# Shifted weight buffers in one layer, stepped and reversed reads on TensorE in the other

## The chip, the cores and the metric

The kernel runs on one core of one Trainium2 chip. Its TensorE (PE) multiplies a stationary operand of 128 columns, which a weight load (PEld) brings in, by a moving operand that streams past it, and adds into PSUM. VectorE (DVE) and ScalarE (ACT) do the elementwise work, and SyncE (SP) issues all the DMAs. The metric is the device time of one execution in microseconds, taken as the median of the runs shown; lower is better.

## The reference

Two layers over x of 256 tokens by 1024 features, all float32, with two residual sums in each. Cut to what matters:

```python
h = rms_norm(x, norm1_g)
q, k, v, iq, ik, iw, a_in, c_in, g_in = split(h @ w_in)      # w_in: 1024 x 9288
y_attn = dsa_attention(rope(norm(q)), rope(norm(k)), v, rope(iq), rope(ik), iw) @ w_attn_out
a = causal_dwconv(a_val * sigmoid(a_gate), conf_conv_w) + conf_conv_b          # 31 taps
y_conf = silu(layer_norm(a)) @ w_conf_out
y_sc = (c_b * causal_dwconv(c_c * c_x, sc_conv_w)) @ w_sc_out                  # 3 taps
x = x + (gate0 * y_conf + gate1 * y_attn + gate2 * y_sc) @ w_o
u = causal_dwconv(rms_norm(x, norm2_g) @ w_up, ffn_conv_w) + ffn_conv_b        # 1024 x 5632
x = x + (silu(u_gate) * u_val) @ w_down                                        # 2816 x 1024
```

## The kernel before

Activations lie with features on the partitions: a tile such as `hh` is 128 x 8 x 256 (partition, block of 128 features, token). Weights arrive as one long stream of chunks of 128 x 2048 floats (1 MB). Each half chunk of 1024 columns, eight weight tiles of 128 columns, is split into two float32r parts: ACT casts the raw half into `wh` (L421, `cast`), and DVE writes the rest, raw less `wh`, into `wl` (L378). There are six buffers of each, `wh_0` to `wh_5` and `wl_0` to `wl_5`, laid out one after the other, and a half is named by its running number (`wh204`). Activations are split in the same way (`hh` and `hl`, `sh` and `sl`, and so on).

A product is three matmuls for each block of 128 features: high weight by high activation, low weight by high activation, high weight by low activation. `fm` (L361 issues them all) writes these, and `pair` makes two output blocks of it (2 x 8 x 3 = 48 matmuls), `single` one (8 x 3 = 24, or 22 x 3 = 66 in the last stage). In these stages the weights are stationary and 256 columns of tokens move. In the stages of `tok` (IQ, KX, V, Q) the roles are swapped: 128 token columns of `hh` or `hl` are stationary and 512, 328 or 256 columns of `wh` or `wl` move.

The stages of a layer, in order, are A (8 pairs; the first of them on `xgh` and `xgl`, before the norm's factor is known, five pairs in layer 0 and three in layer 1, then on `hha` and `hla`), IQ, KX, V, Q, C (8 pairs) with CB (4 pairs), S (4 pairs), G (12 pairs), T (4 pairs), F (4 pairs), O (8 singles), U (22 pairs) and N (8 singles). The attention's own small matmuls (is, qk, tp, po) are put in between. A digit behind the letters is the layer: `F1_0` is the first pair of F in layer 1. `Plan.schedule` lists all instructions ahead of time by due times and estimated costs; each engine then follows its list, and nothing is decided on the chip. `late` in `pair` and `single` puts the last blocks of the contraction at the end, for inputs that come late; in F it stands in the first pair alone. `Norm.finish` writes `hh` (ACT) and `hl` (DVE) for a norm.

Of the kernel before, what the change touches and what calls it, by code (L numbers as in the profile page):

```python
# [9 lines left out]
F32 = mybir.dt.float32  # L10
F32R = mybir.dt.float32r
I32 = mybir.dt.int32
AF = mybir.ActivationFunctionType
ALU = mybir.AluOpType
PSUM = bass.MemoryType.PSUM

P = 128
D = 1024
S = 256
KD = 8  # L20
# [3 lines left out]
FT = 22  # L24
# [6 lines left out]
CHUNK = 2048  # L31
# [26 lines left out]
for _n, _w in (("ident", 128), ("caus0", 128), ("caus1", 256), ("cosq", 32), ("sinq", 32),  # L58
# [9 lines left out]
BANKS = ("pm", "pq", "pa")  # L68
LAYOUT = (["gap40"] + [f"big_{i}" for i in range(8)] + [f"att_{i}" for i in range(2)] + ["kT_0", "vt_0"],
          ["gap16"] + [f"{t}_{i}" for i in range(6) for t in ("wh", "wl")])  # L70
LOADS = {AF.Sigmoid: "sigmoid", AF.Exp: "exp", AF.Silu: "silu"}
LAT = {("dve", "dve"): 127, ("dve", "act"): 130, ("act", "act"): 143, ("act", "dve"): 143,
       ("dve", "pe"): 365, ("act", "pe"): 390, ("pe", "dve"): 198, ("pe", "act"): 198, ("pe", "pe"): 0,
# [62 lines left out]
def ap_of(x):  # L136
    return x.ap() if isinstance(x, View) else x
# [6 lines left out]
class Plan:  # L144
# [166 lines left out]
    def emit(self, tc, pools):  # L311
        order = self.schedule()
        size = {}
        for o in order:
            for b in o.allocs:
                if b.tag not in BANKS:
                    n = int(np.prod(b.shape[1:]))
                    size[b.slot] = max(size.get(b.slot, 0), n)
        first = [t for group in LAYOUT for t in group]
        for slot in first + [t for t in size if t not in first]:  # L320
            if slot.startswith("gap"):
                pools[0].tile([P, int(slot[3:].split("_")[0])], F32, tag=slot, name=slot)
            elif slot in size:
                pools[0].tile([P, size[slot]], F32, tag=slot, name=f"home_{slot}")
        for o in order:
            for b in o.allocs:
                b.tile = pools[b.tag in BANKS].tile(b.shape, b.dtype, tag=b.slot, name=b.name)
            o.fn()


# [1 line left out]
def trunk(ctx: ExitStack, tc: tile.TileContext, xt: bass.AP, wst: bass.AP, prm: bass.AP,  # L332
          cst: bass.AP, out: bass.AP):
    nc = tc.nc
# [5 lines left out]
    G = Plan()  # L340
# [85 lines left out]
    def low(o, full, hi):  # L426
        vtt(o, full, hi.bitcast(F32), ALU.subtract)

    def ks(t):
        return [t[:, k, :] for k in range(KD)]  # L430
# [20 lines left out]
    class Stream:  # L451
# [38 lines left out]
            self.c += 1  # L490
            self.pos = 0

        def tiles(self, n):
            res = []
            for _ in range(n):
                i = 2 * self.c + self.pos // HALF
                o = self.pos % HALF
                h, l = self.get(i)
                res.append((h[:, o:o + P], l[:, o:o + P]))
                self.pos += P  # L500
                if self.pos == widths[self.c]:
                    self.skip()
            return res

    W = Stream()
# [54 lines left out]
    def rsqrt_rows(sq, name):  # L560
# [10 lines left out]
        G.hot = False  # L571
        return r

    def fm(ps, tiles, xh, xl, ka, kb, first, last, group=4, kw=None):
        for a in range(ka, kb, group):
            g = []
            for i in range(a, min(a + group, kb)):
                h, l = tiles[i]
                g.append(mm(ps, h, xh[i], first and i == ka, False, S, kw=kw))
                g.append(mm(ps, l, xh[i], False, False, S, kw=kw))  # L580
            clk["t"] += pe(g, due=clk["t"])
        for a in range(ka, kb, 2 * group):
            g = []
            for i in range(a, min(a + 2 * group, kb)):
                g.append(mm(ps, tiles[i][0], xl[i], False, last and i == kb - 1, S, kw=kw))
            clk["t"] += pe(g, due=clk["t"])

    def pair(name, xh, xl, late=0):
        ps = G.buf([P, 2, S], "pm", name)
        w = [W.tiles(KD) for _ in range(2)]  # L590
        if not late:
            for i in range(2):
                fm(ps[:, i, :], w[i], xh, xl, 0, KD, True, True)
        else:
            cut = KD - late
            for i in range(2):
                fm(ps[:, i, :], w[i], xh, xl, 0, cut, i == 0, False, group=1 if i == 0 else 4, kw="s")
            for i in range(2):
                fm(ps[:, i, :], w[i], xh, xl, cut, KD, False, True, kw="s")
        G.due = clk["t"]  # L600
        return ps
# [15 lines left out]

    def single(name, n, xh, xl, late=0):
        ps = G.buf([P, S], "pm", name)
        w = W.tiles(n)  # L620
        if late:
            fm(ps, w, xh, xl, 0, n - late, True, False)
            fm(ps, w, xh, xl, n - late, n, False, True)
        else:
            fm(ps, w, xh, xl, 0, n, True, True)
        G.due = clk["t"]
        return ps

    def tok(name, xh, xl, n, chunks):
        one = n * 2 <= 512  # L630
        if one:
            t = G.buf([P, 2, n], "pm", name)
            ps = [t[:, b, :] for b in range(2)]
        else:
            t = [G.buf([P, n], "pm", f"{name}_{b}") for b in range(2)]
            ps = t
        per = KD // (2 * chunks)
        for c in range(chunks):
            base = 2 * W.c
            for k0 in range(2 * c * per, 2 * (c + 1) * per, per):  # L640
                h, l = W.get(base + k0 // per - 2 * c)
                g = []
                for k in range(k0, k0 + per):
                    o = k % per * n
                    for b in range(2):
                        sl = slice(b * P, (b + 1) * P)
                        st = k == 0 and (b == 0 or not one)
                        g.append(mm(ps[b], xh[k][:, sl], h[:, o:o + n], st, False, n, kw="s"))
                        g.append(mm(ps[b], xh[k][:, sl], l[:, o:o + n], False, False, n, kw="s"))
                        g.append(mm(ps[b], xl[k][:, sl], h[:, o:o + n], False, k == KD - 1, n, kw="s"))  # L650
                clk["t"] += pe(g, due=clk["t"])
            W.skip()
        G.due = clk["t"]
        return t

    class Norm:
# [28 lines left out]
        def finish(self):  # L685
            self.r = rsqrt_rows(self.sq, self.name)
            self.hh = big(f"hh{self.name}", F32R)
            self.hl = big(f"hl{self.name}", F32R)
            for j in range(KD):
                G.due += 700  # L690
                h = t1(f"h{self.name}_{j}")
                vstt(h, xres[:, j, :], self.g[:, j:j + 1], self.r, ALU.mult, ALU.mult)
                act(self.hh[:, j, :], h, AF.Copy)
                low(self.hl[:, j, :], h, self.hh[:, j, :])

        def deferred(self, ps, name):
            t = t2(name)
# [3 lines left out]
        def pairs(self, n, name, evac):  # L701
            ndef = NDEF[name]
            xh, xl = ks(self.xh), ks(self.xl)
            for j in range(n):
                if j == ndef:
                    xh, xl = ks(self.hh), ks(self.hl)
                if j == 0:
                    G.due = clk["t"] + 1500
                    self.finish()
                if name == "A0" and j < 2:  # L710
                    if j == 0:
                        first = first_pairs(name, xh, xl)
                    ps = first[j]
                else:
                    ps = pair(f"{name}_{j}", xh, xl, late=1 if j == 0 else 0)
                evac(j, ps, self if j < ndef else None)
            return xh, xl
# [32 lines left out]
    for l in range(DEPTH):  # L750
# [34 lines left out]
        xh, xl = norm.pairs(8, f"A{l}", a_evac)  # L785
# [61 lines left out]
        for g in range(4):  # L847
# [9 lines left out]
            n = g - 1  # L857
# [230 lines left out]
def _stream(inp, l):  # L1088
# [4 lines left out]
    def m(x, j):  # L1093
        return x[:, :, j * P:(j + 1) * P].reshape(P, -1)

    parts = []
    for j in range(8):
        parts.append(np.concatenate([m(a, j), m(a, 8 + j)], 1))
    if l == 0:
        four = np.concatenate(parts[:2], 1).reshape(P, 4, KD, P).transpose(0, 2, 1, 3).reshape(P, -1)  # L1100
        parts[:2] = [four[:, :CHUNK], four[:, CHUNK:]]
# [6 lines left out]
    for i in range(4):  # L1108
# [1 line left out]
            j = 2 * i + u  # L1110
            parts.append(np.concatenate([m(c, 8 + j), m(c, 16 + j)], 1))
        parts.append(np.concatenate([m(c, 2 * i), m(c, 2 * i + 1)], 1))
    def square(n):
        w = _blocks(inp[n][l])
        for i in range(4):
            parts.append(np.concatenate([m(w, 2 * i), m(w, 2 * i + 1)], 1))

    square("w_sc_out")
    for n in (1, 2, 0):
        for i in range(4 * n, 4 * n + 4):  # L1120
            parts.append(np.concatenate([m(g, 2 * i), m(g, 2 * i + 1)], 1))
    for n in ("w_attn_out", "w_conf_out", "w_o"):
        square(n)
    w = _blocks(inp["w_up"][l])
    for j in range(FT):
        parts.append(np.concatenate([m(w, j), m(w, FT + j)], 1))
    w = _blocks(inp["w_down"][l])
    w = np.concatenate([m(w, j) for j in range(8)], 1)
    for i in range(0, w.shape[1], CHUNK):
        parts.append(w[:, i:i + CHUNK])  # L1130
    return parts


# [66 lines left out]
```

## Time and profile before

| | |
|---|---|
| median of 2 runs | 1061.48 us (1061.26 and 1061.7) |
| the profiled execution | 1060.66 us, of which the span from first to last instruction is 1058.9 us |
| PE busy | 1051.2 us, 8784 matmuls |
| PEld busy | 1036.1 us, 8784 loads |
| DVE, ACT busy | 913.4 us, 702.5 us |
| mean granted TensorE clock | 0.998 of full speed |

[...] What one costs in a stage is the time from one start to the next: a piece of the chain of waits, divided by the number of its matmuls.

### The profile page before, as it was taken

The page shows a single profiled execution, that of the slowest core. Times are in us where ns is not written, and L with a number is a line of the kernel's source. Part 1 is how long each engine was busy: PE and PEld are TensorE (multiplying, and loading weights), DVE is VectorE, ACT ScalarE, POOL GpSimd, SP SyncE. Part 2 cuts the span into 40 slices and gives each one's busy share as a digit, 9 for nine tenths or more (in the row PEclk, how much of TensorE's full clock was granted, in tenths as well). Part 3 has the DMA queues.
Part 4 walks back from the last instruction along what each step waited for, and adds up shares of the span by engine and source line. Part 5 has one row for each costly group of instructions (what it writes and reads, how often), then busy time and mean ns, then how long its engine had stood idle before and what let it go on. Part 6 is the DMA issues. An engine that isn't in the chain of part 4 may idle for free.

```text
span 1058.9 us, 21702 instructions
## 1 busy us (share of the span) xinstructions
PE 1051.2 (99%) x8784; PEld 1036.1 (98%) x8784; DVE 913.4 (86%) x1813; ACT 702.5 (66%) x1242; POOL 0.2 (0%) x4
## 2 busy tenths in 40 slices
PE   8999999999999999999999999999999999999998
PEld 8999999999999999999999999999999999999998
DVE  6999999999987899875689999999998789987642
ACT  6868657896665666664467686588958457666541
POOL 0000000000000000000000000000000000000000
PEclk9999999999999999999999999999999999999999
DMA  7654544435655356555445554643464653555550
GB/s 272 236 204 165 179 173 165 151 125 181 221 201 194 120 199 224 181 197 201 167 162 206 199 165 156 203 155 120 161 238 157 232 191 136 202 200 199 187 191 20
DMA packets 29460, 191.61 MB, mean 181 GB/s; under 512 B 3504, under 2 KB 4784, under 8 KB 7088
## 3 DMA queue, kind: packets, MB, share of 16 engines
q1 hardware_dynamic: 29360, 190.23, 51.8%
q8 instruction: 68, 1.11, 0.4%
q14 instruction: 32, 0.26, 0.1%
HBM read 189.17 MB, written 1.05 MB: 180 GB/s over the span
## 4 chain that ended last, share of the span: by engine, by line
PE 98%; DMA 1%; DVE 0%; SPq 0%; ACT 0%; issue 0%
PE U L361 23%; PE G L361 12%; PE N L361 12%; PE C L361 8%; PE A L361 8%; PE S L361 4%; PE T L361 4%; PE Q L361 4%; PE O L361 4%; PE F L361 4%; PE CB L361 4%; PE IQ L361 2%; PE KX L361 1%; PE V L361 1%; PE qk L361 1%; PE po L361 1%
## 5 line engine op out<-in xcount | busy, mean ns | idle before, releaser
L378 DVE TENSOR_TENSOR wl<-raw,wh 128x1024 fp32r<-128x1024 f32 (+2 forms) x364 | 433.7, 1201 | 68.1 <-ACT wh L421 66.5
L421 ACT CAST wh<-raw 128x1024 fp32r<-128x1024 f32 (+2 forms) x364 | 368.8, 1029 | 160.8 <-PE N L361 40.5
L361 PE MATMUL U<-hhb,wl 128*128 128x256 f32 x576 | 139.0, 281 | 0.0
L361 PE MATMUL U<-hhb,wh 128*128 128x256 f32 x576 | 138.9, 281 | 0.0
L385 DVE SCALAR_TENSOR_TENSOR acc<-a,psb,acc 128x245 f32<-128x245 f32 (+18 forms) x320 | 132.7, 466 | 0.1
L361 PEld LDWEIGHTS U<-hhb,wh 128*128 128x128 f32 x576 | 109.0, 189 | 0.0
L361 PEld LDWEIGHTS U<-hhb,wl 128*128 128x128 f32 x576 | 108.7, 189 | 0.0
L361 PE MATMUL G<-hha,wh 128*128 128x256 f32 x384 | 91.1, 280 | 0.0
L361 PE MATMUL G<-hha,wl 128*128 128x256 f32 x384 | 89.9, 277 | 0.0
L361 PE MATMUL N<-uh,wl 128*128 128x256 f32 x352 | 83.7, 281 | 0.0
L361 PE MATMUL N<-uh,wh 128*128 128x256 f32 x352 | 83.7, 281 | 0.0
L361 PE MATMUL U<-hlb,wh 128*128 128x256 f32 x576 | 79.6, 281 | 0.0
L385 DVE SCALAR_TENSOR_TENSOR u<-U,psb,u 128x255 f32<-128x255 f32 (+1 forms) x144 | 59.7, 476 | 18.2 <-ACT u L416 18.2
L361 PEld LDWEIGHTS U<-hlb,wh 128*128 128x128 f32 x576 | 73.1, 189 | 0.0
L361 PEld LDWEIGHTS G<-hha,wl 128*128 128x128 f32 x384 | 72.2, 188 | 0.3 <-issue 0.2
L361 PEld LDWEIGHTS G<-hha,wh 128*128 128x128 f32 x384 | 72.1, 188 | 0.3 <-issue 0.2
L416 ACT ACTIVATE ct<-a,psb 128x253 f32<-128x253 f32 (+9 forms) x160 | 70.1, 490 | 0.0
L361 PEld LDWEIGHTS N<-uh,wh 128*128 128x128 f32 x352 | 66.6, 189 | 0.0
L361 PEld LDWEIGHTS N<-uh,wl 128*128 128x128 f32 x352 | 66.5, 189 | 0.0
L361 PE MATMUL C<-hha,wh 128*128 128x256 f32 x256 | 61.5, 281 | 0.0
L361 PE MATMUL C<-hha,wl 128*128 128x256 f32 x256 | 60.4, 277 | 0.0
L416 ACT ACTIVATE u<-U,psb 128x256 f32<-128x256 f32 x72 | 37.2, 560 | 34.7 <-PE U L361 34.7
(259 smaller groups left out, 2590.6 us busy)
## 6 DMA issues: line engine op xcount, KB each, us to landing
raw<-in_w SPq DMA_DIRECT2D x174, 1024.0 KB, 4.8
raw<-in_w SPq DMA_DIRECT2D x4, 656.0 KB, 3.9
raw<-in_w SPq DMA_DIRECT2D x8, 256.0 KB, 6.2
out<-xres SPq DMA_DIRECT2D x8, 128.0 KB, 2.2
xres<-in_xt SPq DMA_DIRECT2D x3, 256.0 KB, 6.6
psb<-in_p SPq DMA_DIRECT2D x2, 277.0 KB, 7.0
csb<-in_c SPq DMA_DIRECT2D x1, 304.0 KB, 7.0
xres<-in_xt SPq DMA_DIRECT2D x2, 128.0 KB, 3.1
```

Source lines behind the costliest of these rows:

```text
L361: nc.tensor.matmul(ap_of(o), ap_of(l), ap_of(r), start=st, stop=sp, skip_group_check=bool(kw))
L378: G.add("dve", lambda: nc.vector.tensor_tensor(ap_of(o), ap_of(a), ap_of(b), op=op), [o], [a, b], (c + n) / 0.96)
L385: G.add("dve", lambda: nc.vector.scalar_tensor_tensor(ap_of(o), ap_of(a), ap_of(s), ap_of(b), op0=op0, op1=op1), [o], [a, s, b], (c + n) / ...
L416: nc.scalar.activation(ap_of(o), ap_of(i), f, **{k: ap_of(v) for k, v in kw.items()})
L421: G.add("act", lambda: nc.scalar.copy(ap_of(o), ap_of(i)), [o], [i], width(o) / 1.2 + 94)
```

## The change

Nothing of what is computed changes. Five things do:

- **Layer 0, buffers.** Each `wh_i` and `wl_i` gets 64 floats more, and in layer 0 (halves with a number below `FAR` = 180) the data begin i + 1 floats, that is 4 to 24 bytes, behind the buffer's start. Layer 1 uses the same buffers unshifted.
- **Layer 1, weights.** Where `STEPS` names a stage, a weight tile is no longer 128 neighbouring floats: its columns are read with a step of 2 (F, U), 4 (S, O) or 8 (T) floats. The stream in HBM is woven accordingly (`woven`).
- **Layer 1, the norm before A.** `hha` and `hla` are stored with the tokens of the two halves interleaved (`natural`). In A from the fourth pair on, C, CB and G the 256 moving columns are so read with a step of 2 floats (8 bytes); in IQ, KX, V and Q the 128 stationary columns are (step 2). ACT and DVE write the two tiles with that step.
- **Layer 1, F and N.** The moving columns are read back to front, and PSUM is written back to front (`turn`). The first pair of F loses its `late` order.
- **Other.** The copy into `hh` is a CAST in place of an ACTIVATE in all norms, and the reserved DMA scratch per partition is 4096 bytes, so that the larger buffers fit.

```diff
+STEPS = {"S": 4, "T": 8, "F": 2, "O": 4, "U": 2}
+MOVES = ("F", "N")
+SHIFT = {f"{t}_{i}": i + 1 for t in ("wh", "wl") for i in range(6)}
+FAR = 2 * (10 + 2 + 1 + 4 + 12 + 4 + 12 + 4 + 4 + 4 + 22 + 11)
...
+                if b.slot in SHIFT:
+                    k, n = SHIFT[b.slot] * (int(b.name[2:]) < FAR), b.shape[1]
+                    b.tile = pools[0].tile([P, n + 64], b.dtype, tag=b.slot, name=b.name)[:, k:k + n]
...
-                res.append((h[:, o:o + P], l[:, o:o + P]))
+                k = o // P
+                a = k // step * step * P + k % step
+                e = slice(a, a + step * (P - 1) + 1, step)
+                res.append((h[:, e], l[:, e]))
...
+    def natural(t):
+        return [t[:, k, :].rearrange("p (b a) -> p a b", a=2) for k in range(KD)]
+
+    def turn(v, name):
+        return v[:, ::-1] if stage(name) in MOVES else v
...
-        w = [W.tiles(KD) for _ in range(2)]
-        if not late:
+        w = [W.tiles(KD, STEPS.get(stage(name), 1)) for _ in range(2)]
+        xh, xl = ([turn(v, name) for v in x] for x in (xh, xl))
+        if stage(name) in MOVES:
+            for i in range(2):
+                fm(turn(ps[:, i, :], name), w[i], xh, xl, 0, KD, True, True)
+        elif not late:
...
-                        sl = slice(b * P, (b + 1) * P)
+                        sl = b if stage(name) else slice(b * P, (b + 1) * P)
...
-                act(self.hh[:, j, :], h, AF.Copy)
-                low(self.hl[:, j, :], h, self.hh[:, j, :])
+                hh, hl = (natural(t)[j] if self.name == "a1" else t[:, j, :] for t in (self.hh, self.hl))
+                h = h.rearrange("p (a b) -> p a b", a=2) if self.name == "a1" else h
+                G.add("act", lambda hh=hh, h=h: nc.scalar.copy(ap_of(hh), ap_of(h)), [hh], [h], S / 1.2 + 94)
+                vtt(hl, h, hh.bitcast(F32), ALU.subtract, n=S)
...
-    nc = _bacc.Bacc("TRN2", target_bir_lowering=False, num_devices=1)
+    nc = _bacc.Bacc("TRN2", target_bir_lowering=False, num_devices=1, dynamic_dma_scratch_size=4096)
```

On PE the order of the instructions changes at one place, the first pair of F in layer 1. Before, blocks 0 to 5 of both outputs come first (`cfl` six times for each), and blocks 6 and 7 behind them:

```order
L361 MATMUL T1_3_10875<-al1_9350,wh277_10810 128x256 x8
L361 MATMUL F1_0_10942<-cfh1_10692,wh278_10825 128x256
L361 MATMUL F1_0_10942<-cfh1_10692,wl278_10859 128x256
...
L361 MATMUL F1_0_10942<-cfl1_10703,wh278_10825 128x256 x6
...
L361 MATMUL F1_0_10942<-cfl1_10703,wh279_10862 128x256 x6
...
L361 MATMUL F1_0_10942<-cfl1_10703,wh278_10825 128x256 x2
```

Now all eight blocks of the first output are done before the second begins:

```order
L369 MATMUL F1_0_10942<-cfh1_10692,wh278_10825 128x256
L369 MATMUL F1_0_10942<-cfh1_10692,wl278_10859 128x256
...
L369 MATMUL F1_0_10942<-cfl1_10703,wh278_10825 128x256 x8
L369 MATMUL F1_0_10942<-cfh1_10692,wh279_10862 128x256
L369 MATMUL F1_0_10942<-cfh1_10692,wl279_10896 128x256
...
L369 MATMUL F1_0_10942<-cfl1_10703,wh279_10862 128x256 x8
```

So the last two blocks of `cfh` and `cfl` are wanted at the 13th and 23rd matmul of F and no longer at the 37th and 41st.

On DVE, in the norm ahead of A in layer 1, the order stays and the form of eight instructions changes. Before:

```order
L378 TENSOR_TENSOR hla1_7204<-ha1_0_7174,hha1_7188 128x256
L378 TENSOR_TENSOR hla1_7204<-ha1_1_7176,hha1_7188 128x256
```

Now, in two runs of 128 with a step of 2 floats:

```order
L386 TENSOR_TENSOR hla1_7204<-ha1_0_7174,hha1_7188 128x2x128
L386 TENSOR_TENSOR hla1_7204<-ha1_1_7176,hha1_7188 128x2x128
```

ACT's eight copies into `hha` change in the same way.

## Rows read from the trace of the kernel before

**Rows 1.** The page: busy time by engine, and the span in 40 slices.

```profile
span 1058.9 us, 21702 instructions
PE 1051.2 (99%) x8784; PEld 1036.1 (98%) x8784; DVE 913.4 (86%) x1813; ACT 702.5 (66%) x1242; POOL 0.2 (0%) x4
...
PE   8999999999999999999999999999999999999998
...
PEclk9999999999999999999999999999999999999999
```

**Rows 2.** The chain that ended last, by engine (page).

```profile
PE 98%; DMA 1%; DVE 0%; SPq 0%; ACT 0%; issue 0%
```

**Rows 3.** All waits of PE: for whom, us in total, times, longest.

```profile
PE A L361 <- ACT xgha L416: 3.0, 2, 2.4
PE pw L361 <- DVE avg L521: 1.0, 1, 1.0
PE A L361 <- DVE wl L378: 0.3, 1, 0.3
```

**Rows 4.** The chain in order of time, layer 1: start us, us, what.

```profile
543.12 37.69 PE A L361 x320
...
662.10 5.44 PE CB L361 x48
667.53 10.88 PE C L361 x96
...
711.14 10.91 PE S L361 x96
...
756.61 30.84 PE G L361 x272
...
802.95 21.76 PE T L361 x192
824.71 21.76 PE F L361 x192
846.47 21.76 PE O L361 x192
...
876.51 116.83 PE U L361 x992
993.34 62.20 PE N L361 x528
```

**Rows 5.** The same chain: wider moving operands, layer 0 and layer 1.

```profile
57.34 11.20 PE IQ L361 x48
...
580.80 11.01 PE IQ L361 x48
591.81 7.27 PE KX L361 x48
...
710.28 0.86 PE po L361 x2
```

**Rows 6.** Timeline of PEld, layer 1: loads for matmuls of one column.

```profile
797.12 0.53 PEld L361 LDWEIGHTS msc<-avg,sqc 128*128 128x128 f32 x4
797.58 0.19 PEld L361 LDWEIGHTS G<-hha,wh 128*128 128x128 f32 x1
```

**Rows 7.** Engines in stretches of layer 0: stretch, us, PE, PEld, DVE, ACT busy.

```profile
20.00:57.00 37.00, 36.67 (x312) 36.46 (x311) 35.83 (x65) 27.00 (x45) 0.00 (x0) 1.00 0.62 222
57.00:106.00 49.00, 49.00 (x362) 46.87 (x362) 46.98 (x108) 38.25 (x92) 0.00 (x0) 1.00 0.56 191
106.00:180.00 74.00, 74.00 (x639) 71.97 (x638) 73.65 (x192) 50.17 (x96) 0.00 (x0) 1.00 0.50 170
180.00:284.00 104.00, 104.00 (x868) 101.03 (x867) 100.04 (x203) 80.06 (x147) 0.00 (x0) 1.00 0.49 170
```

**Rows 8.** DVE's largest group by shape, whole span: busy us, mean ns, idle before.

```profile
L378 DVE TENSOR_TENSOR wl<-raw,wh 128x1024 fp32r<-128x1024 f32 x348 | 421.6, 1221 | 60.4 <-ACT wh L421 58.9
```

**Rows 9.** The tile cfl, layer 1: ns min/median/max, first and last start.

```profile
L378 DVE TENSOR_TENSOR cfl<-lu,cfh x8: 414/418/424, 804.3 to 817.9; 128x256 fp32r<-128x256 f32 x8
```

More of the change, by code (lines that the diff above doesn't have):

```diff
@@ L317, in emit @@
                     n = int(np.prod(b.shape[1:]))
-                    size[b.slot] = max(size.get(b.slot, 0), n)
+                    size[b.slot] = max(size.get(b.slot, 0), n + 64 * (b.slot in SHIFT))
         first = [t for group in LAYOUT for t in group]
@@ L326, in emit @@
             for b in o.allocs:
-                b.tile = pools[b.tag in BANKS].tile(b.shape, b.dtype, tag=b.slot, name=b.name)
+                if b.slot in SHIFT:
+                    k, n = SHIFT[b.slot] * (int(b.name[2:]) < FAR), b.shape[1]
+                    b.tile = pools[0].tile([P, n + 64], b.dtype, tag=b.slot, name=b.name)[:, k:k + n]
+                else:
+                    b.tile = pools[b.tag in BANKS].tile(b.shape, b.dtype, tag=b.slot, name=b.name)
             o.fn()
@@ L491, in skip, with tiles @@
             self.pos = 0
-        def tiles(self, n):
+        def tiles(self, n, step=1):
             res = []
@@ L572, in rsqrt_rows, with stage @@
         return r
+    def natural(t):
+        return [t[:, k, :].rearrange("p (b a) -> p a b", a=2) for k in range(KD)]
+    def turn(v, name):
+        return v[:, ::-1] if stage(name) in MOVES else v
+    def stage(name):
+        n = name.split("_")[0]
+        return n[:-1] if n[-1] == "1" else ""
     def fm(ps, tiles, xh, xl, ka, kb, first, last, group=4, kw=None):
@@ L619, in single @@
         ps = G.buf([P, S], "pm", name)
-        w = W.tiles(n)
+        w = W.tiles(n, STEPS.get(stage(name), 1))
+        to = turn(ps, name)
+        xh, xl = ([turn(v, name) for v in x] for x in (xh, xl))
         if late:
-            fm(ps, w, xh, xl, 0, n - late, True, False)
-            fm(ps, w, xh, xl, n - late, n, False, True)
+            fm(to, w, xh, xl, 0, n - late, True, False)
+            fm(to, w, xh, xl, n - late, n, False, True)
         else:
-            fm(ps, w, xh, xl, 0, n, True, True)
+            fm(to, w, xh, xl, 0, n, True, True)
         G.due = clk["t"]
@@ L706, in pairs @@
                     xh, xl = ks(self.hh), ks(self.hl)
+                    if self.name == "a1":
+                        xh, xl = natural(self.hh), natural(self.hl)
                 if j == 0:
@@ L1094, in m, with woven @@
         return x[:, :, j * P:(j + 1) * P].reshape(P, -1)
+    def woven(parts, name):
+        step = STEPS.get(name, 1)
+        if l == 0 or step == 1:
+            return parts
+        res = []
+        for p in parts:
+            p = p.reshape(P, -1, step, P)
+            res.append(p.transpose(0, 1, 3, 2).reshape(P, -1))
+        return res
     parts = []
@@ L1098, in _stream @@
         parts.append(np.concatenate([m(a, j), m(a, 8 + j)], 1))
+    parts = woven(parts, "A")
     if l == 0:
@@ L1112, in _stream, with square @@
         parts.append(np.concatenate([m(c, 2 * i), m(c, 2 * i + 1)], 1))
-    def square(n):
+    def square(n, name):
         w = _blocks(inp[n][l])
-        for i in range(4):
-            parts.append(np.concatenate([m(w, 2 * i), m(w, 2 * i + 1)], 1))
-    square("w_sc_out")
+        parts.extend(woven([np.concatenate([m(w, 2 * i), m(w, 2 * i + 1)], 1) for i in range(4)], name))
+    square("w_sc_out", "S")
     for n in (1, 2, 0):
@@ L1121, in _stream @@
             parts.append(np.concatenate([m(g, 2 * i), m(g, 2 * i + 1)], 1))
-    for n in ("w_attn_out", "w_conf_out", "w_o"):
-        square(n)
+    for n, name in (("w_attn_out", "T"), ("w_conf_out", "F"), ("w_o", "O")):
+        square(n, name)
     w = _blocks(inp["w_up"][l])
-    for j in range(FT):
-        parts.append(np.concatenate([m(w, j), m(w, FT + j)], 1))
+    parts.extend(woven([np.concatenate([m(w, j), m(w, FT + j)], 1) for j in range(FT)], "U"))
     w = _blocks(inp["w_down"][l])
     w = np.concatenate([m(w, j) for j in range(8)], 1)
-    for i in range(0, w.shape[1], CHUNK):
-        parts.append(w[:, i:i + CHUNK])
+    parts.extend(woven([w[:, i:i + CHUNK] for i in range(0, w.shape[1], CHUNK)], "N"))
     return parts
```

## The prediction

> **What bounds the kernel now.** I read the page first. [...] The chain that ended last is 98% PE [rows 2], and PE waits for other engines 4.3 us in all, at the start [rows 3]. So the time is the number of matmuls times the pace of each stage, and what matters is what the change does to that pace.
>
> The pace is read from the chain in order of time. A matmul of 256 columns costs 37.69/320 = 117.8 ns in A, 30.84/272 = 113.4 in G, 21.76/192 = 113.3 in T, F and O, 10.88/96 = 113.3 in C, 5.44/48 = 113.3 in CB, 10.91/96 = 113.6 in S, and 117.8 in U (116.83/992) and N (62.20/528) [rows 4]. [...]
>
> [...] If what is fetched is neighbouring bytes, a step of 2 makes half of them useless.
>
> **The change part by part.** Sums are made against the profiled execution, 1060.66 us (span 1058.9 and 1.76 around it), 0.8 us under the median of 1061.48.
>
> *Moving columns with step 2* (A from the fourth pair, C, CB, G of layer 1). These are 5 x 48 = 240, 8 x 48 = 384, 4 x 48 = 192 and 12 x 48 = 576 matmuls, 1392 in all. No row shows a stepped stream. From below the cost is nothing, if only the elements read count (a gain is excluded: no column fewer is streamed). From above, 256 columns now span the 2048 bytes that 512 neighbouring ones spanned, and IQ's price for that is 229.4 to 233.3 ns [rows 5]. [...] That adds 240 x (229.4 - 117.8) = 26.8, 384 x 116.1 = 44.6, 192 x 116.1 = 22.3 and 576 x 116.0 = 66.8 us: **+160.5 us**, all on the path, since PE is the path.
>
> *Weights with step 4 or 8* (S, T, O of layer 1: 3 x 192 = 576 loads). The load for the next matmul runs under the present one, and PEld is as busy as PE [rows 1]. Packed weights loaded for matmuls of one column follow each other at (797.58 - 797.12)/4 = 115 ns [rows 6], so a packed load needs at most that, about what a matmul leaves it. From below the step costs nothing, if loads go by words. From above, if the piece that is fetched is four floats long, each column with a step of 4 lies in a piece of its own: 128 columns span 2048 bytes, IQ's 229.4 ns again, now for the load, and the matmul waits for it. [...] A step of 8 touches no more such pieces. That is 192 x (115.8 + 116.1 + 116.1) = **+66.8 us**.
>
> [...]
>
> *Weights with step 2* (U 1056, F 192, V and Q 240, IQ and KX 96). They span 1024 bytes, as the moving 256 columns do at 113 to 118 ns: the load is as long as the matmul, so I take nothing; the bound is U's pace up to 4.5 ns higher, 5 us. In IQ and KX the longer matmul covers it.
>
> *Back to front* (F 192, N 528). The same bytes in the other order, each piece still used whole: nothing; the upper bound is a doubled pace, 192 x 113.3 + 528 x 117.8 = 84 us.
>
> *Shifted buffers, layer 0.* [...] DVE is nearly full there, 256.5 of 264 us in the four stretches [rows 7], and writes `wl` at 1221 ns each [rows 8]; with 7.5 us of slack it covers a few ns on each.
>
> *The rest.* Eight CASTs and eight subtractions with step 2 ahead of A: even at twice the 418 ns of a subtraction of this size [rows 9], DVE loses 8 x 0.42 = 3.3 us, while A's first three pairs (144 x 117.8 = 17 us) run on `xgh` and `xgl`. The lost `late` order in F: `cfl` is last begun at 817.9 [rows 9], F starts at 824.71 [rows 4], and T now takes 22 us longer: nothing. SP's DMAs are the same in number, size and order, and a slower PE leaves them more time.
>
> Sum: 160.5 + 66.8 = 227.3, so 1060.7 + 227.3 = **1288 us**. With the path's prices between 226.7 (twice 113.3) and 233.3, and 5 us for step 2 weights, this case lies at 1282 to 1301.
>
> **The rivals.** What counts as no change is within 2%, 1040 to 1083 us; two runs lie within 0.04%, so a shift of that size is seen.
>
> 1. *Words, not bytes, are fetched.* [...] Then no step costs, and the time is 1061. [...] Against it: nothing in a row. It decides if C1 keeps 113 ns. Here the result is not slower. The two paces of 113.3 and 117.8 for equal work could also change places: 3936 matmuls in A, U and N of both layers by 4.5 ns are 17.7 us, so 1043 at best, which is 1.7%. Chance 0.20.
> 2. [...] Chance 0.09.
> 3. *Only the moving stream is limited.* Loads do not show a limit of their own: 115 ns with one-column matmuls may be start-up, or the pieces are shorter. Then 1060.7 + 160.5 = 1221 us. Chance 0.16.
> 4. *Reversal pays too.* [...] Chance 0.09. [...]
> 5. *Step 2 weights pay as step 4.* 1056 x 112 (U), 192 x 116 (F) and 240 x 114 (V, Q) ns more are 168 us: 1456. Or a stepped access costs more than its bytes. Chance 0.08.
>
> A smaller rival in layer 0: odd-word shifts (half of the slots) slow `wl`. More than 7.5 us over the 90 halves to the end of G, 83 ns or 7% each, and PE waits. At a quarter more on the 45 odd ones (0.3 us each, 13.7 us) that is 6 us, added to any case.
>
> **How the numbers follow.** My forecast (both streams limited by 16-byte pieces) has 0.38. It is the likeliest, so the predicted time is 1288. The range reaches from 1058, which takes in rival 1 as it stands, to 1375, which takes in rival 4; outside are rival 5 and a faster outcome of rival 1, some 0.1. It is wide because the two largest unknowns are each all or nothing; the likeliest case's own range is 1280 to 1302. Slower by over 2%: 0.38 + 0.09 + 0.16 + 0.09 + 0.08 = 0.80. Within 2%: 0.18. Faster: 0.02.
>
> **What would show it.** In the chain after, C1, CB1, G1 and A1 from its fourth pair should pace at 227 to 233 ns, S1, T1 and O1 as well, with U1, F1 and N1 at 113 to 118, and layer 0 unchanged to a microsecond or two. DVE and ACT should show more idle time in layer 1. [...] A wait of PE for `wl` in layer 0 would show the smaller rival.

## The result, and the profile after

The changed kernel takes 1300.47 us (median of 2 runs, 1299.95 and 1301.0) where the kernel before takes 1061.48: a ratio of 1.2252, with an interval of 1.2199 to 1.2304. It is slower by 239 us; forecast were 1288 us, with a range of 1058 to 1375.

First the page of the changed kernel. It answers to [rows 1].

```profile
span 1298.2 us, 21702 instructions
PE 1291.3 (99%) x8784; PEld 1245.8 (96%) x8784; DVE 919.3 (71%) x1813; ACT 704.1 (54%) x1242; POOL 0.2 (0%) x4
...
PE   8999999999999999999999999999999999999999
...
DVE  7999999988799875655975554655443464898752
...
PEclk9999999999999999999999999999999999999999
```

PE has as many matmuls as before and is busy for 240 us longer. The mean granted clock is 0.998 of full speed before and 1.000 after. DVE and ACT work about as long as before, and pause more: DVE falls from 86% to 71%, and its slices from the 21st on show where. All waits of PE are these (for whom, us in total, times, longest); they answer to [rows 3]:

```profile
PE A L369 <- ACT xgha L424: 1.7, 2, 1.1
PE pw L369 <- DVE avg L532: 1.0, 1, 1.0
PE A L369 <- DVE wl L386: 0.9, 1, 0.9
```

They come to 3.6 us, after 4.3 before. So no wait was added: the matmuls themselves follow each other more slowly. The chain in order of time (start us, us, what), layer 1, shows in which stages; it answers to [rows 4, 5]:

```profile
546.87 64.47 PE A L369 x320
...
721.14 11.01 PE CB L369 x48
732.15 22.02 PE C L369 x96
...
813.48 22.28 PE S L369 x96
...
898.06 62.55 PE G L369 x272
...
989.94 46.20 PE T L369 x192
1036.14 22.61 PE F L369 x192
1058.75 45.22 PE O L369 x192
...
1112.55 119.06 PE U L369 x992
1231.61 63.37 PE N L369 x528
```

Divided by the number of matmuls:

| stage of layer 1 | what the change does there | ns per matmul, before | after |
|---|---|---|---|
| CB, C | moving step 2 | 113.3 | 229.4 |
| G | moving step 2 | 113.4 | 230.0 |
| A (240 of the 320) | moving step 2 | 117.8 | 229.4 |
| S, O | weight step 4 | 113.6, 113.3 | 232.1, 235.5 |
| T | weight step 8 | 113.3 | 240.6 |
| U | weight step 2 | 117.8 | 120.0 |
| F | weight step 2, back to front | 113.3 | 117.8 |
| N | back to front | 117.8 | 120.0 |

The figure for A takes the other 80, which read `xgh` and `xgl`, at the old 117.8: (64.47 - 9.42)/240.

Added up over a whole stage from the starts of its matmuls in the two traces, the 239.3 us of longer span are: A +26.6, C +43.9, CB +22.1, G +66.6, together **159.3** (step 2, moving); S +22.3, T +24.5, O +23.5, together **70.2** (step 4 and 8, weights); U +2.5, N +1.2, F +0.9, the stages from IQ to Q +1.2; and layer 0 **+3.7**: G, C, Q, CB and S are longer by 2.1, 1.3, 0.7, 0.6 and 0.3, and A, U, N, F and O together shorter by 1.4. The rest, 0.4, is in the small matmuls.

### The profile page after: what moved, and what is told of

Read it like the earlier page. It is cut to its first block, busy times and chain, and to the rows that moved or that the text cites. A ratio compares the mean times of both kernels' runs of the same rounds, so it can differ in the third digit from the quotient of the medians.

```text
span 1298.2 us, 21702 instructions
## 1 busy us (share of the span) xinstructions
PE 1291.3 (99%) x8784; PEld 1245.8 (96%) x8784; DVE 919.3 (71%) x1813; ACT 704.1 (54%) x1242; POOL 0.2 (0%) x4
## 4 chain that ended last, share of the span: by engine, by line
PE 98%; DMA 1%; ACT 0%; DVE 0%; SPq 0%; issue 0%
PE U L369 19%; PE G L369 15%; PE C L369 10%; PE N L369 10%; PE A L369 8%; PE T L369 5%; PE O L369 5%; PE S L369 5%; PE CB L369 5%; PE Q L369 4%; PE F L369 3%; PE IQ L369 2%; PE KX L369 1%; PE V L369 1%; PE qk L369 1%; PE po L369 1%
## 5 line engine op out<-in xcount | busy, mean ns | idle before, releaser
L369 PE MATMUL G<-hha,wh 128*128 128x256 f32 x384 | 129.1, 356 | 0.0
L369 PE MATMUL G<-hha,wl 128*128 128x256 f32 x384 | 128.2, 354 | 0.0
L369 PE MATMUL C<-hha,wh 128*128 128x256 f32 x256 | 84.5, 349 | 0.0
L369 PE MATMUL C<-hha,wl 128*128 128x256 f32 x256 | 83.7, 346 | 0.0
L369 PEld LDWEIGHTS G<-hha,wl 128*128 128x128 f32 x384 | 76.2, 198 | 4.5 <-issue 0.2
L369 PEld LDWEIGHTS G<-hha,wh 128*128 128x128 f32 x384 | 75.9, 198 | 4.2 <-issue 0.2
L369 PE MATMUL G<-hla,wh 128*128 128x256 f32 x384 | 76.5, 356 | 0.0
L369 PEld LDWEIGHTS G<-hla,wh 128*128 128x128 f32 x384 | 64.0, 198 | 5.5 <-issue 1.4
```

The costliest lines, as they stand in the source:

```text
L369: nc.tensor.matmul(ap_of(o), ap_of(l), ap_of(r), start=st, stop=sp, skip_group_check=bool(kw))
```

## The experiments

Every kernel below is the changed kernel with edits, shown against it. In all but e1, e5 and e9 the columns of `tok` and the lines of `Norm` that interleave are put back as before; these lines, and those that only empty `STEPS` or `MOVES` or set `SHIFT` to 0, are left out of most diffs. In e5, e6 and e9 the stepped reads pick other columns than the computation wants; the amount of work is the same. All keep the longer weight buffers and the CAST, which by themselves do not move the pace of layer 0: U there has 117.8 ns in e1, e2 and e3 as before. In the expectations the theories are called by letters: P is the forecast's estimate (both streams fetch pieces of 16 bytes, some 1.8 ns each, as IQ's 229.4 ns [rows 5] over the 128 such pieces in its 2048 bytes; that pieces are fetched, and their length, were assumed), Q says that neighbouring pairs suffice, and D that the distance between the addresses of weights and moving data counts. The kernel before took 1060.06, 1060.61 and 1059.49 us beside the three groups (e1 to e4, e5 to e8, e9 to e12). Each experiment but e7 is a single run, and seven runs of the kernel before, beside e5 to e8, lie between 1060.07 and 1062.43 us: differences of a few us are read from the chain, stage by stage, and not from the total.

### The four parts, each alone

**e1_moving**: only the interleaved activations stay.

```diff
-STEPS = {"S": 4, "T": 8, "F": 2, "O": 4, "U": 2}
-MOVES = ("F", "N")
-SHIFT = {f"{t}_{i}": i + 1 for t in ("wh", "wl") for i in range(6)}
+STEPS = {}
+MOVES = ()
+SHIFT = {f"{t}_{i}": 0 for t in ("wh", "wl") for i in range(6)}
```

> Only the interleaved hha and hla of layer 1 stay (moving columns with step 2 in A, C, CB, G; stationary columns with step 2 in IQ, KX, V, Q); no shift, no weight steps, no reversal, buffers padded as in the changed kernel. Theory P (the stream fetches pieces of 16 bytes, about 1.8 ns each, so step 2 halves its rate, whatever the loads do): C1, CB1, G1 and A1 from its fourth pair at 229 to 230 ns a matmul, all other stages at 113 to 118, together about 1060.7 + 159 = 1220 us. Rival R (the slow pace comes of the stepped stream and the stepped or shifted weight loads together): nearer 113 in these stages, total well under 1200.

Measured: 1216.65 us, +156.6. Its chain, layer 1:

```profile
727.63 22.02 PE C L369 x96
...
871.12 62.55 PE G L369 x272
...
962.99 22.62 PE T L369 x192
...
1039.27 112.44 PE U L369 x992
1151.71 59.85 PE N L369 x528
```

C and G cost to the hundredth what they cost after, so the first term is this part's alone. T now takes 117.8 ns and U and N 113.3, the reverse of before, though nothing in these three was changed: the same packed work has two paces. The chains show a place where it passes from one to the other, at the small matmuls put in between. Here are the first 35 matmuls of U in layer 1, before and then in e1:

```profile
868.23 3.98 PE U L361 x35
```

```profile
1030.84 4.12 PE U L369 x35
```

They run at 113.7 ns before and at 117.7 in e1. Behind them come `msb`, 29 more of U and `prb`, and then the other 992, at 117.8 before [rows 4] and at 113.3 in e1. So a stage can change its pace midway, and which one it gets depends on what ran earlier: e1 and e2 differ in stages ahead of U alone, and those 992 take 113.3 ns in e1 and 117.8 in e2. Why was not found.

**e2_weights**: only the weight steps, with 8 and 4 changed over between S and T; `tok` and `Norm` as before.

```diff
-STEPS = {"S": 4, "T": 8, "F": 2, "O": 4, "U": 2}
+STEPS = {"S": 8, "T": 4, "O": 4}
...
```

> Only the weight steps of S, T and O stay, and S and T change places: S step 8, T step 4, O step 4. Theory P: a load with each column in a piece of its own takes about 128 pieces of 1.8 ns, so S1, T1 and O1 run at 230 to 241 ns, the rest at 113 to 118; total about 1060.7 + 70 = 1131 us. If a step of 8 costs more than one of 4, S1 is now at 240 to 241 and T1 at 234 to 236; if the 241 of T belonged to the stage, T1 stays at 241 and S1 at 234 to 236. Rival R (only together with other changes): 1061.

Measured: 1136.13 us, +76.1. Chain:

```profile
717.77 23.05 PE S L369 x96
...
830.20 45.23 PE T L369 x192
...
897.20 45.23 PE O L369 x192
```

T at step 4 now costs what O does, 235.6 ns, and S at step 8 240.1. So the 5 to 8.5 ns that T paid more belong to the step of 8, not to the stage.

**e3_rev_u2**: only the reversal in F and N (with F's lost `late` order), and step 2 in U.

```diff
-STEPS = {"S": 4, "T": 8, "F": 2, "O": 4, "U": 2}
+STEPS = {"U": 2}
-SHIFT = {f"{t}_{i}": i + 1 for t in ("wh", "wl") for i in range(6)}
+SHIFT = {f"{t}_{i}": 0 for t in ("wh", "wl") for i in range(6)}
...
```

> Only the reversal of F and N and the weight step of 2 in U stay (F's weights are packed). Theory P: each piece is still used whole or by half at the rate of the load, so next to nothing: N1 at 118 to 120, F1 at 113 to 120, U1 at 118 to 122, total 1060 to 1067 us. Rival (the small rise of U and N in the changed kernel came from the state that the stages before left behind, not from the step and the reversal): U1 and N1 at 117.8 again, total 1061.

Measured: 1062.93 us, +2.9. Chain:

```profile
801.99 21.76 PE T L369 x192
823.75 22.61 PE F L369 x192
846.37 21.77 PE O L369 x192
...
876.72 119.05 PE U L369 x992
995.77 62.20 PE N L369 x528
```

N back to front takes 62.20 us, the same as packed in [rows 4]. U pays 2.2 ns a matmul, 2.5 us in all. F has 117.8, the slower of the two packed paces, between T at 113.3 and O at 113.4. In e1 F has 117.8 without a reversal, but there T and O have it too. So the reversal or the lost `late` order may be what costs F its 0.9 us; no run has a stage that is reversed and runs at 113.3.

**e4_shift**: only the shifted buffers of layer 0 (`STEPS = {}`, `MOVES = ()`).

> Only the shift of the weight buffers by 4 to 24 bytes in layer 0 stays. Theory P with alignment (the pace of a stage depends on where the weights lie against the moving columns): layer 0 as in the changed kernel, halves in the slot shifted by 12 bytes at 113.3 to 113.8 ns, those shifted by 4, 8, 16 and 20 at 118 to 120; layer 1, unshifted, at 113.3 or 117.8 by stage; total 1061 to 1067 us. Rival (VectorE writes wl more slowly off its alignment): wl in layer 0 clearly over 1221 ns and PE waiting for it.

Measured: 1065.17 us, +5.1. Layer 1 is as before. In layer 0 the chain has, first before, then with the shift:

```profile
144.28 10.88 PE C L361 x96
...
234.25 35.38 PE G L361 x312
...
355.67 116.84 PE U L361 x992
```

```profile
146.53 11.31 PE C L369 x96
...
238.46 36.50 PE G L369 x312
...
361.19 116.32 PE U L369 x992
```

G pays 3.6 ns a matmul, and U gains 0.5. DVE is not the cause; its largest group by shape (busy us, mean ns, idle before) is

```profile
L386 DVE TENSOR_TENSOR wl<-raw,wh 128x1024 fp32r<-128x1024 f32 x348 | 420.7, 1219 | 61.7 <-ACT wh L429 60.4
```

against 1221 ns in [rows 8]. Sorted by the buffer in which the weights lie, the mean distances between starts in U of layer 0 are 118.4, 118.3, **113.5**, 118.8, 120.0 and **113.8** ns for shifts of 4, 8, 12, 16, 20 and 24 bytes. Unshifted, it is 117.7.

The four alone add up to 156.6 + 76.1 + 2.9 + 5.1 = 240.7 us, and the whole change costs 239.0: what the parts do to each other is no more than the two paces can make. The step of 2 in F was not run alone.

### Is it pieces of 16 bytes?

**e6_weights3**: weights with a step of 3 in S, T and O. 128 columns then touch 96 pieces of 16 bytes, between the 64 of step 2 and the 128 of step 4.

```diff
-STEPS = {"S": 4, "T": 8, "F": 2, "O": 4, "U": 2}
+STEPS = {"S": 3, "T": 3, "O": 3}
...
-                a = k // step * step * P + k % step
+                a = k // step * step * P + k % step if step != 3 else min(o, HALF - 3 * P)
...
```

> Only weight steps, in S, T and O of layer 1, of 3 floats each; a step of 3 does not divide the half chunk, so the columns read there are not the right ones, and the output of layer 1 is not the reference's; the work is the same. Theory P (pieces of 16 bytes): 128 columns over 1536 bytes are 96 pieces, three quarters of the 128 of step 4, so S1, T1 and O1 at about 96 x 1.82 = 175 ns, total about 1060 + 35 = 1095 us. Rival Q (a load holds its rate while two columns are at most 8 bytes apart, and halves at any larger step): 235 ns, 1130 us. Rival (free up to 12 bytes): 113 to 120 ns, 1061 us.

Measured: 1089.01 us. Chain:

```profile
814.15 33.28 PE T L369 x192
...
870.05 33.28 PE O L369 x192
...
911.76 112.44 PE U L369 x992
1024.20 59.85 PE N L369 x528
```

T and O take 173.3 ns. Per piece of 16 bytes that is 173.3/96 = 1.81 ns, and step 4 has 235.5/128 = 1.84. With pieces of 8 bytes a step of 3 would already cost what a step of 4 does, and with pieces of 32 a step of 8 would cost about twice as much as 4, where it has 240.6. For weight loads pieces of 16 bytes fit these times.

**e5_moving4**: the moving columns with a step of 4. By P each column then needs a piece of its own, and 256 of them some 459 ns.

```diff
-        return [t[:, k, :].rearrange("p (b a) -> p a b", a=2) for k in range(KD)]
+        return [t[:, k, :].rearrange("p (b a) -> p a b", a=4) for k in range(KD)]
...
```

> As e1_moving, but the tokens of four quarters are interleaved: the 256 moving columns of A (from the fourth pair), C, CB and G in layer 1 are read with step 4 (16 bytes) in place of 2. The stationary columns of IQ, KX, V and Q are read with step 2 as in e1_moving, which now picks other tokens, so layer 1's attention works on tokens in a wrong order; the work is the same. Theory P (pieces of 16 bytes, one each 1.8 ns): every column lies in a piece of its own, 256 pieces, so about 459 ns a matmul in these stages, and 1217 + 1392 x 0.23 = 1537 us. Rival Q (two neighbouring columns are taken at once, and any other step goes one by one): 229 ns again, 1217 us. With pieces of 8 bytes also 229.

Measured: 1223.06 us. Chain:

```profile
730.99 22.40 PE C L369 x96
...
876.34 63.46 PE G L369 x272
```

233.3 ns, 4 more than with step 2 and half of what P asks: **P falls for the moving stream**.

**e9_pairs**: the moving columns as neighbouring pairs, with 8 bytes left out behind each. If pairs are what is fetched, this costs as little as packed.

```diff
-        return [t[:, k, :].rearrange("p (b a) -> p a b", a=2) for k in range(KD)]
+        return [t[:, k, :].rearrange("p (b a c) -> p a b c", a=2, c=2) for k in range(KD)]
...
```

> As e1_moving, but hha and hla of layer 1 interleave the two halves by pairs of tokens: the moving columns of A (from the fourth pair), C, CB and G come as two neighbouring floats, then a hop of 16 bytes. IQ, KX, V and Q read 128 neighbouring columns, which are other tokens, so layer 1's attention works on tokens in a wrong order; the work is the same. Theory Q (the stream takes two columns at once where they are neighbours, wherever the next two lie): 113 to 118 ns in these stages, 1061 us. Theory P (pieces of 16 bytes, of which half are now useless): 229 ns, 1217 us.

Measured: 1216.01 us. Chain:

```profile
727.12 22.02 PE C L369 x96
...
870.61 62.55 PE G L369 x272
```

The same 229.4 and 230.0 ns as with step 2: Q falls. P gives the same number here, but e5 has already taken it away. Step 2, step 4 and pairs all cost about 0.9 ns a column (229.4 to 233.3 ns over 256), twice the 0.44 to 0.46 of the packed stream (113.3 to 117.8), and a step of -1 costs 0.46 (117.8 in N, e3). What the stream needs in order to run at that stays open: the three slow patterns have in common that the innermost run of neighbours is one or two columns long, and also that they are read in more than one dimension. A packed operand in two dimensions, or runs of 4 and 8, would have told these apart and were not tried.

### The two packed paces and the shift

**e7_shift12**: all twelve weight buffers shifted by 12 bytes, in both layers, and nothing else of the change (`STEPS = {}`, `MOVES = ()`, `tok` and `Norm` as before).

```diff
-SHIFT = {f"{t}_{i}": i + 1 for t in ("wh", "wl") for i in range(6)}
+SHIFT = {f"{t}_{i}": 3 for t in ("wh", "wl") for i in range(6)}
...
-                    k, n = SHIFT[b.slot] * (int(b.name[2:]) < FAR), b.shape[1]
+                    k, n = SHIFT[b.slot], b.shape[1]
...
```

> No steps and no reversal; all weight buffers, in both layers, begin 12 bytes behind the slot's start. Theory A (where the weights lie against the moving columns sets the pace, as the slot shifted by 12 bytes showed in e4_shift with 113.7 ns, where its neighbours had 118 to 120): all stages with 256 moving columns of activations at 113.3 to 113.8 ns; A, U and N of both layers, T, F and O of layer 0 gain some 4 ns each, about 4500 matmuls, so 1040 to 1046 us. Rival S (the pace of 113 or 118 is a state that is left by what ran before, and the slot only had it by chance): 1055 to 1066 us.

Measured over 4 runs: **1040.14 us** (1039.44 to 1040.86), a ratio of 0.9807 to the kernel before, with an interval of 0.979 to 0.9823. It beats both kernels. Chain:

```profile
298.50 21.76 PE F L369 x192
...
350.20 112.44 PE U L369 x992
462.65 59.84 PE N L369 x528
530.67 36.28 PE A L369 x320
...
861.45 112.44 PE U L369 x992
```

Each of these runs at 113.3 to 113.4 ns, as theory A asks: where the weights are stationary, the slower pace is gone from all long stretches. Q, where they move, has 116.7 throughout, in place of 113.4 and 117.8 before. U gains 4.5 us in each layer, N 2.3, A 1.7, F, O and T of layer 0 0.7 to 0.9 each.

**e8_shifts**: the shift is `SHIFT[b.slot] + (6 if int(b.name[2:]) < FAR else 12)`, that is 28 to 48 bytes by buffer in layer 0 and 52 to 72 in layer 1.

> No steps and no reversal; the six slots are shifted by 28 to 48 bytes in layer 0 and by 52 to 72 bytes in layer 1 (4 bytes more from slot to slot). Theory A: each slot has a pace of its own that depends on the shift alone, between 113 and 121 ns, and some slot may be under 113.3; total 1045 to 1070 us. Rival S: no order by slot.

Measured: 1086.5 us, over the 1045 to 1070 that were expected. No shift among these gives 113; by buffer the mean distances in U of layer 0 lie between 117.5 and 122.1 ns.

**e10_relative** and **e11_relative24**: is it the distance to the moving data? The weights are unshifted, and the activations start 52 or 40 bytes later, so that the weights lie as far from them, counted in 64 bytes, as with a shift of 12 or 24. The edit of e10 (10 in place of 13 in e11):

```diff
...
+                if b.slot.split("_")[0] in ("big", "att"):
+                    n = int(np.prod(b.shape[1:]))
+                    t = pools[0].tile([P, n + 64], b.dtype, tag=b.slot, name=b.name)
+                    b.tile = t[:, 13:13 + n].rearrange("p (a b) -> p a b", a=b.shape[1])
...
```

> Weights unshifted; instead the activation buffers (the moving columns of A, C, CB, S, G, T, F, O, U, N) begin 52 bytes behind their slots in both layers, so that weights lie 12 bytes ahead of them modulo 64, as in e7_shift12. Theory D (the distance between weights and moving columns modulo 64 sets the pace): 113.3 to 113.8 ns in all of these stages, about 1040 us, as e7_shift12. Rival W (where the weights themselves begin within 16 or 32 bytes sets it): not 113.3 throughout; 1055 to 1070 us.

> As e10_relative with 40 bytes in place of 52, so that weights lie 24 bytes ahead of the moving columns modulo 64 and both begin on 8 bytes. Theory D: the pace that the slot shifted by 24 bytes had in e4_shift, 114.2 ns, in all stages with moving activations, 1041 to 1048 us. Rival W: 1055 to 1070 us.

Measured: 1116.84 and 1102.25 us. U in the chain of e10, then of e11:

```profile
924.57 122.33 PE U L373 x992
```

```profile
912.61 120.43 PE U L373 x992
```

The other long stretches with stationary weights have the same, 123 and 121.4 ns: D falls, and rival W, with 1055 to 1070 us for both, missed the times too. Where the activations begin matters by itself, and at the two other places tried it was worse.

**e12_shift24**: `SHIFT` is 6 for all buffers, 24 bytes, in both layers.

> As e7_shift12 with all weight buffers 24 bytes behind their slots in both layers. Both theories on the pace expect the slot's 114.2 ns of e4_shift in all stages, 1041 to 1048 us; if the slot had that pace only in its neighbourhood of other slots, 1050 to 1065 us.

Measured: 1056.3 us. Chain:

```profile
302.05 21.76 PE F L369 x192
...
353.82 115.73 PE U L369 x992
469.55 61.60 PE N L369 x528
```

F runs at 113.3, U and N at 116.7. In e4 the buffer with 24 bytes had 113.8 in U, so a buffer's own shift is not all that counts: theory A foresaw the pace at 12 bytes and missed it at 24. Why 12 bytes are good and others not was not found.

## Why the prediction was right, and where not

- **What bounds the kernel** held: the time is the number of matmuls times the pace of each stage, no wait appeared (3.6 us in all, after 4.3), and the mean granted clock was 1.000 of full speed, after 0.998.
- **Moving step 2, 160.5 us forecast**: 159.3 measured, and 156.6 for the whole kernel when alone (e1, where U and N also got the better pace, -6.6 us, and T, F and O the worse, +2.6). IQ's price for the same span of bytes gave the right number.
- **Its reason failed.** The step that failed is the one that reads both streams as fetching pieces of 16 bytes, some 1.8 ns each, which was the author's estimate. For the moving stream a step of 4 would then double the price again, and it costs 4 ns more (233.3, e5). No run shows the limit on fetching for which 229.4 ns were taken for the moving columns and put on the loads of step 4 and 8; what the runs showed in its place is 229.4 to 230.0 ns for the moving columns, and 232.1 to 235.5 at step 4 and 240.6 at step 8 for the weights. That the number came out all the same is luck: at step 2, twice the bytes and half the rate make the same price, and the forecast could not tell one from the other. What halves the rate stays open.
- **Weights, step 4 and 8, 66.8 us forecast**: 70.2. The piece of four floats that was assumed fits: 1.81 ns a piece at a step of 3 (173.3/96, e6) and 1.84 at 4 (235.5/128). Mis-sized is the price per piece, 1.84 ns for a load in place of the 1.79 of IQ's moving stream (229.4/128), and the sentence that a step of 8 touches no more pieces: it does not, and it pays 5 ns more all the same.
- **Weights, step 2, nothing forecast, at most 5 us**: 2.5 us in U (e3), inside the bound. The stages from IQ to Q of layer 1 together lost 1.2 us.
- **Back to front, nothing forecast**: nothing in N in e3, which took 62.20 us either way, and at most 0.9 us in F, where the lost order is not told apart from it. After, N has 120.0 ns; e3 shows that this is not the reversal by itself. Nor is it simply left over from U: in e3 U has 120.0 just ahead as well, and N has 117.8. What makes it stays open.
- **F's lost order, nothing forecast**: `cfl` is last begun at 1015.1 in the trace after (ns min/median/max, first and last start):

```profile
L386 DVE TENSOR_TENSOR cfl<-lu,cfh x16: 415/418/424, 294.3 to 1015.1; 128x256 fp32r<-128x256 f32 x16
```

  F starts at 1036.14 and waits for nothing. Its +0.9 us are the slower packed pace.
- **Shifted buffers, nothing in the sum, and layer 0 expected unchanged to a microsecond or two**: 3.7. C and G, where the shifted buffer is stationary and only loaded, go from 116.6 and 115.7 ns to 119.9 and 119.2 in the mean of layer 0 (e4, and the same after).
- **DVE's odd words, the smaller rival**: nothing, `wl` took 1219 ns (e4).

The 12 us between forecast and result are thus 3.4 from the weight steps, 3.7 from the shift, 2.5 from U and 3.3 from the small changes of pace in F, N and IQ to Q, less 1.2 on the moving step, and 0.4 in the small matmuls. Of the rivals, 1 and 3 each left out a term that is there (1 C at 229.4, both T at 240.6), 4 and 5 added one that is not (N at 120.0, U at 120.0 after). The forecast noted that the two paces could change places for up to 17.7 us; that they can be set, by 12 bytes, was not foreseen.

## What to carry to other kernels

In a kernel whose chain is all PE, price a layout by the pace of each stage, from start to start, and take a bound for an unknown stream from a row that covers the same bytes; but keep the price and its reason apart. One run with a second step size tests the reason: here the bytes covered gave the price at step 2, and would have given twice the measured one at step 4. In this kernel the float32r moving columns are best left neighbours throughout: step 2 took a matmul of C from 113.3 to 229.4 ns, and so did pairs (e9), while a step of 2 on the weight side cost 2.2 ns of 118, and reversing the moving columns and the output cost nothing in N, which ran at the slower packed pace. Where packed matmuls show two paces, try starting the weight buffers a few words later: 12 bytes were worth 1.9% here, 24 bytes 0.3%, and 28 to 72 bytes cost 2.4% (four runs of the first, one of each of the others).

## What the runs showed of the hardware that was not expected

- Weight loads of 128 float32r columns set the pace by their step: 120.0 ns at 2 (U), 173.3 at 3, 235.5 at 4, 240.6 at 8. Moving streams of 256 columns: 229.4 at 2, 233.3 at 4, 229.4 as pairs, and at -1 117.8 in N (e3), as packed there. At a step of 2 the moving side cost 229.4 ns and the weight side 120.0.
- Equal packed matmuls run at 113.3 or at 117.8 ns, and untouched stages change from one to the other when an earlier stage is changed (T, U and N in e1; U and N in e6, 117.8 to 113.3). U of layer 1 changed over midway, at the small matmuls put in between (113.7 to 117.8 before, 117.7 to 113.3 in e1).
- Where operands begin, counted in words, moves the packed pace between 113.3 (weights 12 bytes later) and 123.3 ns (activations 52 bytes later), with waits of PE of 3.2 and 4.8 us in all, 4.3 before, and a granted clock of 1.000 and 0.998.
